# Small products of two heads interleaved on the two halves of the TensorE array, in a two-layer hybrid decoder kernel

## The chip, the cores and the metric

The kernel runs on one core of one Trainium2 chip. Its time is the device time of one execution in microseconds (us), the median of several runs. A profile of one more execution gives the rows that are read below; there, PE is TensorE's matrix products, PEld its weight loads, DVE is VectorE, ACT is ScalarE, POOL is GpSimd and SP is the queue that issues the transfers.

## The reference, cut to what matters

Two layers of a decoder for 256 tokens of width 1024. In each layer four token mixers work on one projected input, and each has four heads of 64 channels:

```
xn = rmsnorm(h);  u_nsa, u_hgrn, u_ret, u_rwkv = split(xn @ w_in)
nsa:   per head, scores q.k against 16 compressed blocks, 256 selected and 256 window keys;
       three softmaxes, each with a causal mask, times their values
hgrn:  S_t = diag(f_t) S_(t-1) + k_t^T v_t ;  o_t = q_t S_t        (per head, 64 x 64 state)
ret:   (q k^T * decay) v                                            (per head)
rwkv:  S_t = S_(t-1)(diag(w_t) - kk^T (kk a)) + v_t^T k_t ; y_t = S_t r_t
h = h + (sum_m sigmoid(xn @ w_gate[m]) * (mixer_m @ w_branch[m])) @ w_out
h = h + (silu(hn @ w_ffn_gate) * (hn @ w_ffn_up)) @ w_ffn_down
h = h + sigmoid(hp @ w_ple_gate) * (p @ w_ple_proj)
```

## The kernel before

Channels lie on the 128 partitions and tokens along the free side; a chunk of 128 channels holds two heads, the even head (`hp` = 0) on partitions 0 to 63 and the odd one (`hp` = 1) on 64 to 127. There are two kinds of products.

The **big products** (lines L222 to L224, L264 to L266, L440 to L442) are the projections: each float32 weight block is loaded, split into a high and a low part by ACT (L207) and DVE (L208), and multiplied in three products of 128x128 weights with 256 columns. They need nothing of the mixers except at a few places, and fill TensorE for most of the time.

The **small products** are the mixers' own, in float32. All of them are issued by the helper `matmul` or `transpose` of `Front` and so carry its line, L141 (L144 issues nothing itself). A float32 product that is no transpose runs as two records in the trace. A small product uses a part of the array, given by `tile_position`: rows (the partitions of its operands) and columns (the partitions of its result). A product of 64 channels uses one half of the rows; one whose result is on 64 partitions, one half of the columns; one with both, a quarter.

The order of the instructions on each engine is made when the kernel is built, by a scheduler with priorities: there are three lanes, "G" for the big products, "A" for rwkv and "B" for ret, hgrn and nsa. `Front` puts a small product 100000 ahead in priority, so that it goes before any big product once the scheduler takes it for ready. On the chip each engine runs its list in order. Results go to 8 PSUM banks: two named `pA` (lane A), three `pB` (lane B), three `mm` (big products). A new tile of a name waits for one of its banks to be read out.

The small products that the change touches, in the order of a layer: in `rwkv` the sums of squares `pk` (two products of 32 result rows), the four chunk products per head into `pa` (`[128, 4, 128]`, one bank a head), and the transposed values `pv` (8 products on the halves of the columns, the four of one half first); in `hgrn` the blocks of `hgrn_blocks` (8 quarter products a head, called once with 64 columns and three times, over `hq`, with 96), four quarter products a head into `pp`, and two of 128 columns a head into `pp` for the off-diagonal part; in `nsa` the scores of a head (`nsa_scores`: bank `pb` with 272 and 16 columns, each a product and then a mask added by a bfloat16 product of `nmx` with the identity on the whole array; bank `pa` with two products of 256 columns and a mask), and the eight transposes of `nsa_turn`.

Of the kernel before, what the change touches and what calls it, by code (L numbers as in the profile page):

```python
# [32 lines left out]
P = 128  # L33
# [96 lines left out]
class Front:  # L130
# [7 lines left out]
    def _issue(self, f, *args, **kw):  # L138
        p = self.tc.cur_priority
        self.tc.cur_priority = p - self.AHEAD  # L140
        f(*args, **kw)  # L141
        self.tc.cur_priority = p + 1

    def matmul(self, *args, **kw):  # L144
        self._issue(self.nc.tensor.matmul, *args, **kw)

    def transpose(self, *args, **kw):
        self._issue(self.nc.tensor.transpose, *args, **kw)


class Trunk:
# [372 lines left out]
    def rwkv(self, l, ums):  # L524
# [44 lines left out]
        for j in range(2):  # L569
            self.pe.matmul(pk[32 * j:32 * j + 32], self.hsel, sq[:, j], start=True, stop=True, tile_position=(0, 32 * j))  # L570
# [37 lines left out]
        for j in range(2):  # L608
            for hp in range(2):
                h = 2 * j + hp  # L610
                hr = slice(hp * 64, hp * 64 + 64)
                pa = self.ps([P, 4, 128])
                for c in range(4):
                    self.pe.matmul(pa[:, c], bk[c % 2][hr, j, c // 2].rearrange("p x t -> p (x t)"),
                                     ar[c % 2][hr, j, c // 2].rearrange("p x t -> p (x t)"), start=True, stop=True)
# [58 lines left out]
        for par in range(2):  # L674
            for cp in range(2):
                c = 2 * cp + par
                for j in range(2):
# [122 lines left out]
    def hgrn(self, l, tm, zs):  # L800
# [32 lines left out]

        for hp in range(2):
            pp = self.ps([P, 4, 64])
            self.hgrn_blocks(hp, k, lambda jc, x: q[64 * hp:64 * hp + 64, jc // 2, (jc % 2) * P + 64 * x:(jc % 2) * P + 64 * x + 64], pp)
            V.tensor_mul(cd[hp], pp, self.id64[:, None, :].to_broadcast([P, 4, 64]))
# [4 lines left out]
        for i, m in enumerate(QUADS):  # L842
# [25 lines left out]
            V.tensor_mul(quad(kn)[:, :, :3], kb[:, :, :3], bc(post))  # L868
            for hp in range(2):
                pp = self.ps([P, 4, 96])  # L870
                self.hgrn_blocks(hp, k, lambda jc, x: qq[64 * hp:64 * hp + 64, 2 * jc + x], pp)
# [6 lines left out]

        for hp in range(2):
            hr = slice(hp * 64, hp * 64 + 64)  # L880
            pp = self.ps([P, 2, 2, 64])
            for jc in range(4):
                j, c = jc // 2, jc % 2
                self.pe.matmul(pp[:64, j, c], k[hr, j, c * P:c * P + 64], q[hr, j, c * P + 64:c * P + P],
                                 start=True, stop=True, tile_position=(64 * hp, 0))
            nc.scalar.activation(at[hp][:64, :, :, 64:], pp[:64], AF.Copy)
# [10 lines left out]
        V.tensor_mul(half(kn)[:, :, 0], half(k)[:, :, 0], bc(1))  # L897
        for hp in range(2):
            hr = slice(hp * 64, hp * 64 + 64)
            pp = self.ps([P, 2, P])  # L900
            for j in range(2):
                self.pe.matmul(pp[:, j], kn[hr, j, :P], qn[hr, j, P:], start=True, stop=True)
            nc.scalar.activation(ato[:, hp], pp, AF.Copy)
# [3 lines left out]
    def hgrn_blocks(self, hp, k, q, out):  # L907

        for jc in range(4):
            for x in range(2):  # L910
                ts = slice((jc % 2) * P + 64 * x, (jc % 2) * P + 64 * x + 64)
                self.pe.matmul(out[64 * x:64 * x + 64, jc], k[64 * hp:64 * hp + 64, jc // 2, ts], q(jc, x),
                                      start=True, stop=True, tile_position=(64 * hp, 64 * x))
# [66 lines left out]
    def nsa(self, l, tm, vc, ksw, q):  # L980
# [6 lines left out]
        es, ts = [], []  # L987
        for step in "ssTsTpsTTp":
# [10 lines left out]

# [49 lines left out]
    def nsa_turn(self, ea, e2, ec):  # L1049
# [6 lines left out]
        for br in range(2):  # L1056
            self.pe.transpose(p2[:, br], ea[:, 1, br], self.ident)
# [412 lines left out]
```

## Time and profile before

| | us |
|---|---|
| median of 3 runs | 1031.58 (1031.05 to 1031.73) |
| the profiled execution | 1034.5 |
| its span, first to last instruction | 1032.7 |
| PE busy in the span | 1016.8 (98%), 9548 products |
| DVE busy | 770.4 (75%) |
| ACT busy | 541.1 (52%) |
| mean granted TensorE clock | 0.993 |

A busy figure is the time that an engine's records cover. Records of PE overlap, as a product is in flight while the next begins; the time that a product holds up its followers is therefore read from start to start, not from its length. The mixers of the first layer lie between 35 and 216 us of the span, those of the second between 542 and 724.

### The profile page before, as it was taken

To read this page: it belongs to the slowest core of one execution; us is meant where nothing else is said; L and a number is where in the kernel's file an instruction comes from. 1 tells how busy PE (TensorE), PEld (TensorE's weight loads), DVE (VectorE), ACT (ScalarE), POOL (GpSimd) and SP (SyncE) were. 2 spreads that over 40 slices of the span, in tenths; PEclk is the share of its full clock that TensorE was granted. 3 is DMA by queue.
4 is the path that set the end of the run, shared out by engine and by line. 5 is a ranking of instruction groups with operands and counts; after the bars stand their busy time and mean duration, and the time that the engine had idled before them with its cause. 6 is when DMAs were issued, how large, how long until landed. Compare 5 with 4: busy or idle time off the path is not lost.

```text
span 1032.7 us, 22828 instructions
## 1 busy us (share of the span) xinstructions
PE 1016.8 (98%) x9548; PEld 976.8 (95%) x9548; DVE 770.4 (75%) x1337; ACT 541.1 (52%) x863; POOL 7.6 (1%) x28
## 2 busy tenths in 40 slices
PE   8999999999999999999999999999999999999996
PEld 8988988899999999999998989988999999999996
DVE  6888968687787777656767889576777777776566
ACT  6643554565664544455545545546456544544444
POOL 0000000000000000000000000000000000000000
PEclk9999999999999999999989999999999999999998
DMA  8654333246665666666644553333566666666661
GB/s 289 188 198 146 103 104 94 91 155 201 186 203 182 189 197 192 185 192 197 181 157 126 184 165 104 101 105 93 172 200 181 182 192 196 193 196 184 191 184 55
DMA packets 50502, 171.33 MB, mean 166 GB/s; under 512 B 5856, under 2 KB 6624, under 8 KB 50272
## 3 DMA queue, kind: packets, MB, share of 16 engines
q1 hardware_dynamic: 50112, 169.76, 53.8%
q8 instruction: 75, 1.23, 0.5%
q14 instruction: 27, 0.22, 0.1%
q10 hardware_dynamic: 288, 0.11, 0.0%
HBM read 168.80 MB, written 1.05 MB: 164 GB/s over the span
## 4 chain that ended last, share of the span: by engine, by line
PE 88%; DVE 7%; DMA 2%; issue 2%; ACT 1%; SPq 0%; DVEq 0%; ACTq 0%
PE mm L222 22%; PE mm L223 21%; PE mm L224 21%; PE pB L141 6%; PE pA L141 5%; DVE wl L208 2%; PE pA L222 2%; PE pA L223 2%; PE pA L224 2%; DMA T<-in_w_cmp_dram 1%; PE pA L264 1%; PE pA L265 1%; PE pA L266 1%; DMA cst<-in_consts_dram 1%; PE pB L364 1%
## 5 line engine op out<-in xcount | busy, mean ns | idle before, releaser
L207 ACT ACTIVATE wh<-wr 128x1024 fp32r<-128x1024 f32 (+3 forms) x314 | 325.8, 1040 | 355.1 <-PE mm L224 223.9
L208 DVE TENSOR_TENSOR wl<-wr,wh 128x1024 fp32r<-128x1024 f32 (+3 forms) x314 | 375.0, 1196 | 143.2 <-ACT wh L207 141.4
L222 PE MATMUL mm<-xh,wl 128*128 128x256 f32 x1472 | 411.8, 280 | 0.9 <-DVE lbw L1186 0.7
L224 PE MATMUL mm<-xh,wh 128*128 128x256 f32 x1472 | 410.6, 279 | 0.0
L223 PE MATMUL mm<-xl,wh 128*128 128x256 f32 x1472 | 410.6, 279 | 0.0
L222 PEld LDWEIGHTS mm<-xh,wl 128*128 128x128 f32 x1472 | 276.7, 188 | 4.4 <-issue 1.4
L223 PEld LDWEIGHTS mm<-xl,wh 128*128 128x128 f32 x1472 | 276.6, 188 | 2.9 <-issue 2.1
L224 PEld LDWEIGHTS mm<-xh,wh 128*128 128x128 f32 x1472 | 276.8, 188 | 2.5 <-issue 1.4
L222 PE MATMUL mm<-A,wl 128*128 128x256 f32 x332 | 91.8, 277 | 0.0
L223 PE MATMUL mm<-A,wh 128*128 128x256 f32 x332 | 91.8, 277 | 0.0
L224 PE MATMUL mm<-A,wh 128*128 128x256 f32 x332 | 91.8, 277 | 0.0
L222 PEld LDWEIGHTS mm<-A,wl 128*128 128x128 f32 x332 | 62.5, 188 | 0.0
L224 PEld LDWEIGHTS mm<-A,wh 128*128 128x128 f32 x332 | 62.3, 188 | 0.0
L223 PEld LDWEIGHTS mm<-A,wh 128*128 128x128 f32 x332 | 62.3, 188 | 0.0
L141 PE MATMUL pA<-A,A 64*64 64x64 f32 (+3 forms) x1008 | 49.7, 223 | 1.1 <-DVE A L648 1.1
L141 PEld LDWEIGHTS pA<-A,A 64*64 64x64 f32 (+3 forms) x1008 | 41.6, 135 | 8.8 <-DVE A L648 1.5
L222 PE MATMUL mm<-Y,wl 128*128 128x256 f32 x160 | 44.7, 279 | 0.0
L223 PE MATMUL mm<-Y,wh 128*128 128x256 f32 x160 | 44.4, 277 | 0.0
L224 PE MATMUL mm<-Y,wh 128*128 128x256 f32 x160 | 44.2, 276 | 0.0
L1230 DVE TENSOR_TENSOR T<-mm,rstd 128x512 f32<-128x512 f32 x32 | 22.1, 689 | 13.9 <-PE mm L224 13.9
L1233 ACT ACTIVATE T<-T,vech 128x256 f32<-128x256 f32 x64 | 28.8, 500 | 2.6 <-DVE T L1230 2.6
L222 PEld LDWEIGHTS mm<-Y,wl 128*128 128x128 f32 x160 | 30.1, 188 | 0.0
(388 smaller groups left out, 1612.5 us busy)
## 6 DMA issues: line engine op xcount, KB each, us to landing
wr<-in_w_gate_dram SPq DMA_DIRECT2D x64, 512.0 KB, 3.7
wr<-in_w_fm_dram SPq DMA_DIRECT2D x46, 512.0 KB, 4.3
wr<-in_w_fg_dram SPq DMA_DIRECT2D x44, 512.0 KB, 4.2
wr<-in_w_fu_dram SPq DMA_DIRECT2D x44, 512.0 KB, 4.1
wr<-in_w_fd_dram SPq DMA_DIRECT2D x32, 512.0 KB, 3.8
wr<-in_w_branch_dram SPq DMA_DIRECT2D x16, 512.0 KB, 4.3
wr<-in_w_out_dram SPq DMA_DIRECT2D x16, 512.0 KB, 4.1
wr<-in_w_pg_dram SPq DMA_DIRECT2D x16, 512.0 KB, 4.2
```

The costliest lines, as they stand in the source:

```text
L141: f(*args, **kw)
L207: nc.scalar.activation(hi[:, s], raw[:, s], AF.Copy)
L208: nc.vector.tensor_sub(lo[:, s], raw[:, s], hi[:, s])
L222: mm(out, wlo, xhi, start=start, stop=False)
L223: mm(out, whi, xlo, start=False, stop=False)
L224: self.last_mm = mm(out, whi, xhi, start=False, stop=stop)
L264: mm(ps[:, c], lo, xs[k][0], start=c == 0 and k == 0, stop=False, skip_group_check=True)
L265: mm(ps[:, c], hi, xs[k][1], start=False, stop=False, skip_group_check=True)
L266: mm(ps[:, c], hi, xs[k][0], start=False, stop=k == n - 1, skip_group_check=True)
L364: nc.tensor.matmul(ps[:, tc_:tc_ + 1], a[:, tc_ * P:(tc_ + 1) * P], self.inv_dm, start=i == 0 and tc_ == 0, stop=i == n - 1, skip_group_ch ...
L1230: self.nc.vector.tensor_mul(th, ps, self.rstd_b)
L1233: self.nc.scalar.activation(th[:, c], th[:, c], AF.Tanh, scale=0.5, bias=self.vech[l][:, col:col + 1])
```

## The change

`Front.together` issues a list of products as one group: the first is issued, and the scheduler is told to take the others right after it. The lists go through both heads in turn (odd head, even head, odd head, ...), each head into a bank of its own, and begin with the product whose operand is made last. `hgrn_blocks` now makes both heads' blocks and returns both banks. The `pv` products change halves of the columns with each product. In nsa the bank `pb` is started once, by the 272-column product, where it was started twice; the 16-column product and the two masks follow; this opening part, now `nsa_first`, is made for head h+1 in one list with the rest of head h. The transposes of `nsa_turn` are one list. No product, no shape and no operation of another engine is added or removed.

```
     def matmul(self, *args, **kw):
-        self._issue(self.nc.tensor.matmul, *args, **kw)
+        return self._issue(self.nc.tensor.matmul, *args, **kw)
...
+    def together(self, steps):
+
+        head = steps[0]()
+        with self.tc.issue_after(head.ins):
+            for f in steps[1:]:
+                f()
...
         pk = self.ps([64, T])
-        for j in range(2):
-            self.pe.matmul(pk[32 * j:32 * j + 32], self.hsel, sq[:, j], start=True, stop=True, tile_position=(0, 32 * j))
+        self.pe.together([functools.partial(self.pe.matmul, pk[32 * j:32 * j + 32], self.hsel, sq[:, j], start=True, stop=True,
+                                            tile_position=(0, 32 * j)) for j in (1, 0)])
...
         for j in range(2):
+
+            pas = [self.ps([P, 4, 128]) for _ in range(2)]
+
+            def chunk(c, hp):
+                hr = slice(hp * 64, hp * 64 + 64)
+                return self.pe.matmul(pas[hp][:, c], bk[c % 2][hr, j, c // 2].rearrange("p x t -> p (x t)"),
+                                      ar[c % 2][hr, j, c // 2].rearrange("p x t -> p (x t)"), start=True, stop=True)
+
+            self.pe.together([functools.partial(chunk, c, hp) for c in (3, 0, 1, 2) for hp in (1, 0)])
             for hp in range(2):
...
-        for par in range(2):
-            for cp in range(2):
-                c = 2 * cp + par
-                for j in range(2):
+        for cp in range(2):
+            for j in range(2):
+                for par in range(2):
+                    c = 2 * cp + par
...
-        for hp in range(2):
-            pp = self.ps([P, 4, 64])
-            self.hgrn_blocks(hp, k, lambda jc, x: ..., pp)
+        pps = self.hgrn_blocks(k, lambda hr, jc, x: ..., 64)
...
+            pps = self.hgrn_blocks(k, lambda hr, jc, x: qq[hr, 2 * jc + x], 96)
...
+        pps = [self.ps([P, 2, 2, 64]) for _ in range(2)]
+        steps = []
+        for jc in range(4):
+            j, c = jc // 2, jc % 2
+            for hp in (1, 0):
+                hr = slice(hp * 64, hp * 64 + 64)
+                steps.append(functools.partial(self.pe.matmul, pps[hp][:64, j, c], k[hr, j, c * P:c * P + 64],
+                                               q[hr, j, c * P + 64:c * P + P], start=True, stop=True, tile_position=(64 * hp, 0)))
+        self.pe.together(steps)
...
+        pps = [self.ps([P, 2, P]) for _ in range(2)]
+        steps = []
+        for j in range(2):
+            for hp in (1, 0):
+                hr = slice(hp * 64, hp * 64 + 64)
+                steps.append(functools.partial(self.pe.matmul, pps[hp][:, j], kn[hr, j, :P], qn[hr, j, P:], start=True, stop=True))
+        self.pe.together(steps)
...
+    def hgrn_blocks(self, k, q, n):
+
+        pps = [self.ps([P, 4, n]) for _ in range(2)]
+        steps = []
         for jc in range(4):
             for x in range(2):
                 ts = slice((jc % 2) * P + 64 * x, (jc % 2) * P + 64 * x + 64)
+                for hp in (1, 0):
+                    hr = slice(64 * hp, 64 * hp + 64)
+                    steps.append(functools.partial(self.pe.matmul, pps[hp][64 * x:64 * x + 64, jc], k[hr, jc // 2, ts], q(hr, jc, x),
+                                                   start=True, stop=True, tile_position=(64 * hp, 64 * x)))
+        self.pe.together(steps)
+        return pps
...
+    def nsa_first(self, h, ksw, q, beside=()):
+
+        j, hr = h // 2, slice((h % 2) * 64, (h % 2) * 64 + 64)
+        pb = self.ps([P, 512])
+        mm = lambda o, w, x, start=False, stop=False: functools.partial(self.pe.matmul, o, w, x, start=start, stop=stop,
+                                                                        skip_group_check=True)
+        steps = [mm(pb[:, :272], q[hr, j, :P], ksw[hr, :272], start=True), *beside[:1],
+                 mm(pb[:, 272:288], q[hr, j, P:], ksw[hr, :16]), *beside[1:],
+                 mm(pb[:, :272], self.identb, self.nmx[:, 16:]),
+                 mm(pb[:, 272:288], self.identb, self.nmx[:, :16], stop=True)]
+        self.pe.together(steps)
+        return pb
...
-        mm(pb[:, :272], q[hr, j, :P], ksw[hr, :272], start=True, stop=False, skip_group_check=True)
-        mm(pb[:, :272], self.identb, self.nmx[:, 16:], start=False, stop=True, skip_group_check=True)
-        mm(pb[:, 272:288], q[hr, j, P:], ksw[hr, :16], start=True, stop=False, skip_group_check=True)
-        mm(pb[:, 272:288], self.identb, self.nmx[:, :16], start=False, stop=True, skip_group_check=True)
...
+        if h < 3:
+            self.first = self.nsa_first(h + 1, ksw, q, steps)
+        else:
+            self.pe.together(steps)
...
+        self.pe.together([tr(p2[:, 1], ea[:, 1, 1]), tr(p2[:, 0], ea[:, 1, 0]), *(tr(p2[:, 2 + c], ec[:, c]) for c in range(2)),
+                          *(tr(p1[:, br, 0], e2[:, br]) for br in range(2)), *(tr(p1[:, br, 1], ea[:, 0, br]) for br in range(2))])
```

What this makes of the order on TensorE is shown at three places of the first layer. A row is one product, or several of the same that follow each other; the numbers behind a name tell tiles apart, and the size is that of the result.

In hgrn, the second use of `hgrn_blocks` on `hq`, on TensorE before (`pB_267` is the even head's bank, `pB_268` the odd one's; `pA` is rwkv, `mm` big products):

```order
L440 MATMUL mm_239_1874<-wl242_1908,xh_173 128x256
L441 MATMUL mm_239_1874<-wh242_1907,xl_174 128x256
L141 MATMUL pA_96_800<-A_95_798,A_92_777 64x64 x16
L141 MATMUL pB_267_2010<-hq_261_1990,B_247_1949 64x96 x8
L141 MATMUL pB_268_2022<-hq_261_1990,B_247_1949 64x96 x8
L442 MATMUL mm_239_1874<-wh242_1907,xh_173 128x256
```

and the same place now:

```order
L142 MATMUL pA_96_800<-A_95_798,A_92_777 64x64 x16
L142 MATMUL pB_268_2011<-hq_261_1990,B_247_1949 64x96
L142 MATMUL pB_267_2010<-hq_261_1990,B_247_1949 64x96
L142 MATMUL pB_268_2011<-hq_261_1990,B_247_1949 64x96
L142 MATMUL pB_267_2010<-hq_261_1990,B_247_1949 64x96
L142 MATMUL pB_268_2011<-hq_261_1990,B_247_1949 64x96
L142 MATMUL pB_267_2010<-hq_261_1990,B_247_1949 64x96
L142 MATMUL pB_268_2011<-hq_261_1990,B_247_1949 64x96
L142 MATMUL pB_267_2010<-hq_261_1990,B_247_1949 64x96
L142 MATMUL pB_268_2011<-hq_261_1990,B_247_1949 64x96
L142 MATMUL pB_267_2010<-hq_261_1990,B_247_1949 64x96
```

The sixteen products of two heads stood one head behind the other and now take turns; the place among the big products is the same.

In rwkv, the chunk products of the second pair of heads (`pA_77` is the even head's bank, `pA_78` the odd one's; `mm` are big products), on TensorE before:

```order
L141 MATMUL pA_77_664<-A_65_620,A_67_622 128x128
L141 MATMUL pA_77_664<-A_66_621,A_68_623 128x128
L141 MATMUL pA_77_664<-A_65_620,A_67_622 128x128
L141 MATMUL pA_77_664<-A_66_621,A_68_623 128x128
L222 MATMUL mm_209_1558<-xh_173,wl210_1561 128x256
L223 MATMUL mm_209_1558<-xl_174,wh210_1560 128x256
L224 MATMUL mm_209_1558<-xh_173,wh210_1560 128x256
L222 MATMUL mm_209_1558<-xh_173,wl210_1561 128x256
L223 MATMUL mm_209_1558<-xl_174,wh210_1560 128x256
L224 MATMUL mm_209_1558<-xh_173,wh210_1560 128x256
L141 MATMUL pA_78_677<-A_65_620,A_67_622 128x128
```

and now:

```order
L142 MATMUL pA_78_665<-A_66_621,A_68_623 128x128
L142 MATMUL pA_78_665<-A_65_620,A_67_622 128x128
L142 MATMUL pA_78_665<-A_66_621,A_68_623 128x128
L142 MATMUL pA_78_665<-A_65_620,A_67_622 128x128
L233 MATMUL mm_209_1558<-xl_174,wh210_1560 128x256
L234 MATMUL mm_209_1558<-xh_173,wh210_1560 128x256
L232 MATMUL mm_209_1558<-xh_173,wl210_1561 128x256
L142 MATMUL pA_77_664<-A_66_621,A_68_623 128x128
L142 MATMUL pA_77_664<-A_65_620,A_67_622 128x128
L142 MATMUL pA_77_664<-A_66_621,A_68_623 128x128
L142 MATMUL pA_77_664<-A_65_620,A_67_622 128x128
L233 MATMUL mm_209_1558<-xl_174,wh210_1560 128x256
```

The two heads still stand apart, with big products between them: the odd head now goes first and the even head three big products later. (For the first pair of heads, whose two banks are both free, the built order does take turns; and the two `pk` products, which had one big product between them, now follow each other.)

In nsa, the scores of the first head, on TensorE before (`pB_309` is `pb`, `pB_308` is `pa`):

```order
L141 MATMUL pB_301_2200<-cst_155,B_300_2198 128x128 x4
L141 MATMUL pB_309_2218<-ns_ksw_207_1552,U_208_1557 128x272
L141 LDWEIGHTS identb_516
L141 MATMUL pB_309_2218<-nmx_518,identb_516 128x272
L141 MATMUL pB_309_2218<-ns_ksw_207_1552,U_208_1557 128x16
L141 LDWEIGHTS identb_516
L141 MATMUL pB_309_2218<-nmx_518,identb_516 128x16
L141 MATMUL pB_308_2217<-ns_ksw_207_1552,U_208_1557 128x256 x2
L141 LDWEIGHTS identb_516
L141 MATMUL pB_308_2217<-nmx_518,identb_516 128x256
```

and now (`pB_308` is `pb` of the first head, `pB_310` that of the second):

```order
L142 MATMUL pB_301_2200<-cst_155,B_300_2198 128x128 x4
L142 MATMUL pB_308_2217<-ns_ksw_207_1552,U_208_1557 128x272
L142 MATMUL pB_308_2217<-ns_ksw_207_1552,U_208_1557 128x16
L142 LDWEIGHTS identb_516
L142 MATMUL pB_308_2217<-nmx_518,identb_516 128x272
L142 LDWEIGHTS identb_516
L142 MATMUL pB_308_2217<-nmx_518,identb_516 128x16
L142 MATMUL pB_310_2223<-ns_ksw_207_1552,U_208_1557 128x272
L142 MATMUL pB_310_2223<-ns_ksw_207_1552,U_208_1557 128x16
L142 LDWEIGHTS identb_516
L142 MATMUL pB_310_2223<-nmx_518,identb_516 128x272
L142 MATMUL pA_127_987<-A_111_905,A_113_920 64x64 x4
```

The two score products of a bank now stand together, with its two masks behind them. The first head's bank `pa` has moved from behind the masks to two big products later, past the second head's opening. The odd heads' openings take turns with the rest of the head before only for the last pair, heads 2 and 3; for the others the built order keeps the two parts apart.

## Rows read from the trace of the kernel before

**Rows 1.** The page, its parts on busy time (engine, us, share of the span, instructions) and on the chain of work that ended last (share of the span by engine).

```profile
PE 1016.8 (98%) x9548; PEld 976.8 (95%) x9548; DVE 770.4 (75%) x1337; ACT 541.1 (52%) x863; POOL 7.6 (1%) x28
...
PE 88%; DVE 7%; DMA 2%; issue 2%; ACT 1%; SPq 0%; DVEq 0%; ACTq 0%
```

**Rows 2.** The waits of TensorE over the whole span: who waited for whom, us in total, times, longest.

```profile
PE mm L141 <- DMA T<-in_w_cmp_dram: 1.9, 2, 1.0
...
PE pA L141 <- DVE A L648: 1.1, 2, 0.6
```

**Rows 3.** Busy time of each engine in stretches of the span (start and end, length; then per engine us busy and instructions, the granted TensorE clock, DMA share, GB/s). The first four lie in the first layer's mixers, the last two are the same places of the second layer as the first two.

```profile
75.00:95.00 20.00, 18.92 (x197) 17.01 (x196) 19.78 (x47) 9.42 (x14) 0.00 (x0) 1.00 0.50 173
115.00:135.00 20.00, 19.43 (x340) 18.15 (x339) 19.81 (x49) 10.83 (x25) 0.30 (x1) 1.00 0.30 96
135.00:155.00 20.00, 20.00 (x285) 17.77 (x279) 10.64 (x26) 12.80 (x26) 0.00 (x0) 1.00 0.33 99
155.00:215.00 60.00, 60.00 (x521) 52.14 (x520) 45.20 (x117) 32.91 (x89) 0.00 (x0) 1.00 0.34 101
583.00:603.00 20.00, 18.99 (x199) 17.16 (x199) 19.75 (x47) 9.42 (x14) 0.00 (x0) 1.00 0.52 174
623.00:643.00 20.00, 19.49 (x350) 18.17 (x348) 19.85 (x50) 11.08 (x25) 0.30 (x1) 1.00 0.33 99
```

**Rows 4.** The order of time on TensorE, small products of 64 rows by 128 columns with 256 moving columns (start, us until the last end, line, names, weights rows*columns, result, type, records): in rwkv, where rows 0 to 63 and 64 to 127 take turns, and in nsa, where all four records use one half. A row's start to the next row's start is what it takes.

```profile
40.22 1.14 PE L141 MATMUL pA<-A,sm 64*128 64x256 f32 x8
41.28 0.38 PE L223 MATMUL mm<-xl,wh 128*128 128x256 f32 x1
...
167.12 1.13 PE L141 MATMUL pB<-ns_ksw,U 64*128 64x256 f32 x4
168.18 0.28 PE L141 MATMUL pB<-nmx,identb 128*128 128x256 bf16 x1
```

**Rows 5.** The order of time on TensorE at the two `pk` products.

```profile
49.48 0.28 PE L222 MATMUL mm<-xh,wl 128*128 128x256 f32 x1
...
50.23 0.38 PE L223 MATMUL mm<-xl,wh 128*128 128x256 f32 x1
50.55 0.62 PE L141 MATMUL pA<-A,cst 128*32 128x256 f32 x2
51.10 0.38 PE L224 MATMUL mm<-xh,wh 128*128 128x256 f32 x1
51.32 0.29 PE L222 MATMUL mm<-xh,wl 128*128 128x256 f32 x1
```

**Rows 6.** The order of time on TensorE at the chunk products of the first pair of heads (`pA<-A,A`), among products of ret on halves of the columns (`pB<-tm,B`), and at those of one later head.

```profile
71.83 0.28 PE L223 MATMUL mm<-xl,wh 128*128 128x256 f32 x1
72.03 0.80 PE L141 MATMUL pB<-tm,B 128*64 128x64 f32 x18
72.76 0.49 PE L141 MATMUL pA<-A,A 64*128 64x128 f32 x4
...
75.36 0.38 PE L224 MATMUL mm<-xh,wh 128*128 128x256 f32 x1
...
78.75 1.16 PE L141 MATMUL pA<-A,A 64*128 64x128 f32 x8
79.84 0.38 PE L222 MATMUL mm<-xh,wl 128*128 128x256 f32 x1
```

**Rows 7.** The order of time on TensorE at three groups of quarter products: hgrn with 64 columns, hgrn over `hq` with 96, and rwkv's 32x32 products with the idle time before them and what ended it.

```profile
115.99 0.97 PE L141 MATMUL pB<-B,B 64*64 64x64 f32 x32
116.89 0.38 PE L442 MATMUL mm<-wh,xh 128*128 128x256 f32 x1
...
122.42 1.22 PE L141 MATMUL pB<-hq,B 64*64 64x96 f32 x31
123.57 0.39 PE L442 MATMUL mm<-wh,xh 128*128 128x256 f32 x1
...
134.66 0.69 PE L141 MATMUL pA<-A,A 32*32 32x32 f32 x32 [0.57 <-DVE A L648]
135.28 0.39 PE L222 MATMUL mm<-xh,wl 128*128 128x256 f32 x1
```

**Rows 8.** The order of time on TensorE where hgrn ends: `pv` (`pA<-cst,A 128*64`), the rest of the third `hq` group, the odd head's quarter products `pp` (`pB<-B,B 64*64`) and the off-diagonal part of the odd head (`64*128`).

```profile
140.48 1.58 PE L141 MATMUL pA<-cst,A 128*64 128x128 f32 x16
141.99 0.62 PE L141 MATMUL pB<-hq,B 64*64 64x96 f32 x9
...
142.53 0.24 PE L141 MATMUL pB<-hq,B 64*64 64x96 f32 x1
...
142.62 0.24 PE L141 MATMUL pB<-hq,B 64*64 64x96 f32 x1
...
143.56 0.68 PE L141 MATMUL pB<-B,B 64*64 64x64 f32 x8
144.17 0.39 PE L223 MATMUL mm<-xl,wh 128*128 128x256 f32 x1
...
147.47 0.71 PE L141 MATMUL pB<-B,B 64*128 64x128 f32 x4
148.11 0.69 PE L141 MATMUL pA<-A,A 128*64 128x64 f32 x16
```

**Rows 9.** The order of time on TensorE at the opening of nsa's first head: its first product; the opening with both products and both masks lasts until the 256-column products of group 4 begin.

```profile
165.81 0.72 PE L141 MATMUL pB<-ns_ksw,U 64*128 64x272 f32 x2
```

More of the change, by code (lines that the diff above doesn't have):

```diff
@@ L608, in rwkv @@
         for j in range(2):
+            pas = [self.ps([P, 4, 128]) for _ in range(2)]
[4 more added lines that the diff above has]
+            self.pe.together([functools.partial(chunk, c, hp) for c in (3, 0, 1, 2) for hp in (1, 0)])
             for hp in range(2):
-                h = 2 * j + hp
+                h, pa = 2 * j + hp, pas[hp]
                 hr = slice(hp * 64, hp * 64 + 64)
[L612 to L615, printed above, removed]
                 for par in range(2):
@@ L877, in hgrn @@
             q, k = qn, kn
-        for hp in range(2):
[L880 to L886, printed above, removed]
+        pps = [self.ps([P, 2, 2, 64]) for _ in range(2)]
[7 more added lines that the diff above has]
+        self.pe.together(steps)
+        for hp in range(2):
+            nc.scalar.activation(at[hp][:64, :, :, 64:], pps[hp][:64], AF.Copy)
             for x in range(2):
@@ L897, in hgrn @@
         V.tensor_mul(half(kn)[:, :, 0], half(k)[:, :, 0], bc(1))
-        for hp in range(2):
[L899 to L903, printed above, removed]
+        pps = [self.ps([P, 2, P]) for _ in range(2)]
[5 more added lines that the diff above has]
+        self.pe.together(steps)
+        for hp in range(2):
+            nc.scalar.activation(ato[:, hp], pps[hp], AF.Copy)
         sms = [(at[h % 2][:, h // 2, 0], ato[:, h % 2, h // 2], at[h % 2][:, h // 2, 1]) for h in range(4)]
         return self.tm_out(l, sms, tm, EPS, False, "Y1", V_HN, None, s2)
-    def hgrn_blocks(self, hp, k, q, out):
+    def hgrn_blocks(self, k, q, n):
+        pps = [self.ps([P, 4, n]) for _ in range(2)]
+        steps = []
         for jc in range(4):
@@ L987, in nsa @@
         es, ts = [], []
+        self.first = self.nsa_first(0, ksw, q)
         for step in "ssTsTpsTTp":
@@ L1052, in nsa_turn @@
         p1, p2 = self.ps([P, 2, 2, P]), self.ps([P, 4, P])
-        for br in range(2):
-            self.pe.transpose(p1[:, br, 0], e2[:, br], self.ident)
-            self.pe.transpose(p1[:, br, 1], ea[:, 0, br], self.ident)
-        for br in range(2):
-            self.pe.transpose(p2[:, br], ea[:, 1, br], self.ident)
-        for c in range(2):
-            self.pe.transpose(p2[:, 2 + c], ec[:, c], self.ident)
+        tr = lambda o, x: functools.partial(self.pe.transpose, o, x, self.ident)
+        self.pe.together([tr(p2[:, 1], ea[:, 1, 1]), tr(p2[:, 0], ea[:, 1, 0]), *(tr(p2[:, 2 + c], ec[:, c]) for c in range(2)),
+                          *(tr(p1[:, br, 0], e2[:, br]) for br in range(2)), *(tr(p1[:, br, 1], ea[:, 0, br]) for br in range(2))])
         ta = self.g([P, 2, 2, P])
```

23 lines of the change are left out of this document (11 added, 12 removed).

## Prediction

> **What bounds the kernel now.** Read first the page's busy times and its chain: TensorE is busy 98% of the span and makes up 88% of the chain, so what it does not have to do comes off the end, unless it then waits [rows 1]. Then TensorE's waits: those that belong to the mixers are few, 1.9 us for the compression weights' transfer and 1.1 us for DVE in an rwkv group, both layers together [rows 2]. Then the engines by stretch. In the first layer DVE is busy 19.78 of 20 us between 75 and 95, and 19.81 of 20 between 115 and 135; the second layer shows 19.75 and 19.85 at the same places. Between 135 and 155 it is busy 10.64 of 20, and between 155 and 215 45.20 of 60 [rows 3]. So TensorE's time is the bound in the later mixers, and in the two tight stretches DVE is one as well. The granted clock is 1.00, the level of 2.4 GHz, in all of these.
>
> **What taking turns is worth.** Eight rwkv records of 256 columns that take turns on the two halves of the rows need 41.28 - 40.22 = 1.06 us until the next product; four nsa records of the same size, all on one half, need 168.18 - 167.12 = 1.06 us [rows 4]. The second half is free. This is the measured form of what the change does, with the same weights (64x128), so I take it for all groups that really take turns, and half the time is the bound that no group can beat.
>
> **The terms, for one layer**, each from start to start. An ordinary big product follows the one before it by 0.11 us (an estimate from the 0.11 to 0.12 between the big products' starts where no small one lies between).
>
> *pk.* From the big product at 49.48 to the one at 51.32 it is 1.84 us, with two visits to small products [rows 5]. One visit: 0.75 (49.48 to 50.23), then 0.22 for the next big one (51.10 to 51.32) and 0.11 for the last: 1.08. The two products go to different columns, so the second is taken as free beside the first. Saved 0.76; if it is not free, 0.24 less, by the 0.55 to 0.75 of a visit.
>
> *Chunk products, first pair of heads.* 71.83 to 75.36, 3.53 us, holds these 16 records and 40 of ret in turns [rows 6]. Sixteen that take turns should need what eight of one head need: 79.84 - 78.75 = 1.09 and 0.20 to enter. The 40: 18 took 0.73, of which 0.20 is the change to another tile size, so 0.029 each, 1.17, and 0.20 to enter and to leave. Together 2.86, less 0.11 as the two groups now have one more big product between them: saved 0.78 here. In the second layer the order still has one mixed visit; I take 0.7 for the mean. The second pair of heads stands apart in the new order, odd head first, even head later: 0.
>
> *hgrn, 64 columns.* 32 records in 0.90 us [rows 7], eight on each quarter of the array. Eight records on one quarter alone take 144.17 - 143.56 = 0.61 [rows 8]. If the quarters are independent, 0.29 is saved.
>
> *hgrn over hq, first and second.* 31 records from 122.42 to 123.57, 1.15 us [rows 7]. On one quarter they follow at 0.09 (142.53, 142.62) [rows 8]; eight are 0.10 + 7 x 0.085, and 0.17 to leave: an estimate of 0.8. Saved 0.4 each, 0.8.
>
> *The end of hgrn.* `pv`: 16 records in 141.99 - 140.48 = 1.51 us, one half of the columns after the other [rows 8]. In turns they are eight at 0.109 (1.51 less 0.20 to leave, over the some 12 that did not overlap) and 0.20: 1.07, saved 0.44. `pp`: the odd head's run of 0.61 lies beside the even head's, saved 0.6. Off-diagonal: 148.11 - 147.47 = 0.64 for the odd head, saved 0.64 [rows 8]. Against it, the new order cuts `pp` into pieces among products of other tile sizes; two extra changes at some 0.15 to 0.2. Net 1.35, bounds 0.9 and 1.7.
>
> *nsa.* Opening a bank takes 167.12 - 165.81 = 1.31 us now [rows 4, 9], with four changes between half and whole array. With one change: 0.33 for a 272-column record, 0.23 for the other, 0.24 for the two small ones and 0.22 for the masks, 1.0; these parts are estimates, 256 columns on one half being 0.22 apart by [rows 4]. Saved 0.3 a head, 1.2. Heads 2 and 3 alone take turns, which puts most of the 1.06 of four 256-column records beside the opening: 0.8. Some gathered transposes: 0.2. Sum 2.2, bounds 1.2 and 2.6.
>
> Sum: 0.76 + 0.7 + 0.29 + 0.8 + 1.35 + 2.2 = 6.1 us a layer, 12.2 in both.
>
> **The rule on weight loads** bears on `pv`. The trace: 18 ret records in turns on two halves of the columns, with all rows, came at 0.029 us after the change of size is taken off [rows 6], below the 0.109 of one half [rows 8]; so loads on the other half of the columns do overlap. The Trainium skill, TensorE: Matmul & The Clock Gate, Part 3 (The mechanism), says that a weight load overlaps a running product only when its row group differs. By that rule `pv` gains nothing and the time would be 0.9 us later over two layers. The trace disagrees, and the sum goes by the trace.
>
> **What is given back.** The stretch from 115 to 135 cannot get shorter than DVE's work in it, 19.81 of 20 us [rows 3]. The two gains there (hgrn 64 columns, hq: 1.1 us) I count as lost to waits on DVE's masks and copies, such as the 0.57 us before the 32x32 products [rows 7]; bounds nothing and all of it. The 1.46 of `pk` and the chunks fall before the stretch from 75 to 95; TensorE comes earlier to a transfer that it already waits for and to a DVE that is full. But DVE has some slack before 75, and the transfer is set off by TensorE's own progress: of 1.46 I take 0.2 as lost (bounds 0 and 1.46). After 135 DVE is half idle and nothing is given back. So 1.3 a layer, 2.6 in both.
>
> 12.2 - 2.6 = 9.6 us. The profiled execution took 1034.5 us, which gives 1024.9; the median of the runs shown is 2.9 lower, and the same saving gives 1031.58 - 9.6 = **1022.0**. With the bounds that are likely together (gain 11 to 13.5, given back 1 to 4.5) the forecast spans 1019 to 1025.
>
> **The rivals.** *Nothing is given back* (0.15): DVE works ahead once results come sooner; the 0.57 us wait was one place only. 1031.6 - 12.2 = 1019.4, and 1018.2 with the upper bound of nsa.
>
> *Banks* (0.17): a group takes two or three banks at once. Lane A has two, lane B three, and a new tile waits until one is read. In nsa all three are taken by `pb` and `pa` of one head and `pb` of the next, so transposes and the next scores wait for the softmax. For it: the order that keeps the second pair of chunk products apart. Against: PE never idles in 155 to 215 [rows 3], where big products fill the holes. Beside it stands a page: the Trainium skill, TensorEngine Tiling (Array Packing), Gotcha 1: PSUM Pressure, states that row tiles write to different banks and that row tiling raises the pressure on PSUM; no run here shows it yet. If nsa's 2.2 and all before 135 but 1.0 go, 1.0 + 1.35 a layer are left: 4.7 in both, 1026.9.
>
> *No change* (0.04): the halves do not run beside each other and only visits saved count; `pk` 0.76 a layer, less waits: 1030 to 1032. [rows 4] speaks against it.
>
> *Slower* (0.05): TensorE's list is in order, and a group begins with the product that is ready last. If the real operand comes later than the scheduler took it to, everything queued behind waits: big products, and with them DVE's and ACT's next results. There are about 17 groups a layer, 34 in all; at 0.28 us more wait each the 9.6 is gone, at 0.36 the time is 1034.2. In the tight stretches this is plausible; elsewhere [rows 2] shows no such waits.
>
> **The numbers.** Forecast 0.59. Faster by over 0.2% (2 us, about what a measurement of this kernel can tell from no change): 0.59 + 0.15 + 0.17 = 0.91. Same 0.04, slower 0.05. The range takes in the first two rivals, 1018.2 and 1026.9, and leaves out about 0.1.
>
> **What would show it.** In the profile after: `pB<-hq,B` groups of 32 records at about 0.8 us; `pB<-B,B 64*128` with eight records in 0.64; nsa's opening at 1.0; the first pair of chunk products 16 records in 1.1; TensorE idle before small products near 115 to 135 longer than the 0.57 us, with DVE named. It is wrong if groups of turns show twice the length of one head, if TensorE waits for DVE or ACT between 155 and 215, or if the big products start later there than the list before would have them.

## The result and the profile after

The changed kernel takes 1024.34 us (median of four executions, 1022.4 to 1027.5) against 1031.65 in the runs beside it: ratio 0.9932, 95% interval 0.9915 to 0.9949, 7.3 us less. Forecast were 1022.0, with a range of 1018.2 to 1026.9. The profiled execution took 1024.59 us, span 1022.8.

The page after, busy time and chain, answers [rows 1]; the waits of TensorE below it (who waited for whom, us in total, times, longest) answer [rows 2]:

```profile
PE 1008.8 (99%) x9548; PEld 975.6 (95%) x9548; DVE 769.3 (75%) x1337; ACT 539.9 (53%) x863; POOL 7.3 (1%) x28
...
PE 89%; DVE 7%; issue 1%; DMA 1%; ACT 1%; DVEq 0%; ACTq 0%
```

```profile
PE pA L142 <- DVE A L663: 1.5, 1, 1.5
...
PE pB L142 <- DVE hq L866: 0.5, 1, 0.5
PE mm L142 <- DMA T<-in_w_cmp_dram: 0.4, 1, 0.4
...
PE pA L142 <- ACT A L674: 0.3, 1, 0.3
```

TensorE is as full as before. Its waits on the mixers came to 1.9 and 1.1 us; now they are 1.5, 0.5, 0.4 and 0.3, a little less in sum, but elsewhere: the compression weights are waited for 1.5 us less, and VectorE 0.9 us more, of whose 2.0 us now 1.48 stand at one place. The stretches that answer [rows 3]:

```profile
115.00:135.00 20.00, 18.52 (x299) 17.52 (x294) 19.81 (x55) 10.85 (x24) 0.30 (x1) 0.96 0.36 107
155.00:215.00 60.00, 60.00 (x538) 54.61 (x537) 46.89 (x119) 34.81 (x90) 0.00 (x0) 1.00 0.36 109
623.00:643.00 20.00, 19.12 (x325) 17.68 (x324) 19.88 (x52) 10.88 (x25) 0.30 (x1) 1.00 0.35 108
```

Between 155 and 215 TensorE never idles (60.00 of 60), so no bank leaves it without work there; before, it did not idle there either. Between 115 and 135 VectorE is busy 19.81 of 20 us, as before, and TensorE now only 18.52. The order of time on TensorE at the groups of [rows 5 to 9]:

```profile
49.08 0.28 PE L232 MATMUL mm<-xh,wl 128*128 128x256 f32 x1
49.28 0.63 PE L142 MATMUL pA<-A,cst 128*32 128x256 f32 x4
49.84 0.38 PE L233 MATMUL mm<-xl,wh 128*128 128x256 f32 x1
50.06 0.28 PE L234 MATMUL mm<-xh,wh 128*128 128x256 f32 x1
50.18 0.29 PE L232 MATMUL mm<-xh,wl 128*128 128x256 f32 x1
...
72.30 1.16 PE L142 MATMUL pA<-A,A 64*128 64x128 f32 x16
73.39 0.38 PE L233 MATMUL mm<-xl,wh 128*128 128x256 f32 x1
...
112.99 0.70 PE L142 MATMUL pB<-B,B 64*64 64x64 f32 x32
113.61 0.38 PE L452 MATMUL mm<-wh,xh 128*128 128x256 f32 x1
...
119.24 0.83 PE L142 MATMUL pB<-hq,B 64*64 64x96 f32 x29
120.00 0.39 PE L452 MATMUL mm<-wh,xh 128*128 128x256 f32 x1
...
131.70 0.69 PE L142 MATMUL pA<-A,A 32*32 32x32 f32 x32 [1.48 <-DVE A L663]
132.33 0.39 PE L232 MATMUL mm<-xh,wl 128*128 128x256 f32 x1
...
138.86 1.09 PE L142 MATMUL pA<-cst,A 128*64 128x128 f32 x16
139.88 0.47 PE L142 MATMUL pB<-hq,B 64*64 64x96 f32 x11
...
163.08 0.85 PE L142 MATMUL pB<-ns_ksw,U 64*128 64x272 f32 x4
...
164.09 0.49 PE L142 MATMUL pB<-ns_ksw,U 64*128 64x272 f32 x1
```

```profile
145.60 0.97 PE L142 MATMUL pB<-B,B 64*64 64x64 f32 x10
146.50 0.39 PE L233 MATMUL mm<-xl,wh 128*128 128x256 f32 x1
```

The row at 145.60 merges two records of `pp` with the eight of the off-diagonal part, the first of which starts at 145.86. The sizes of the groups measured here are those of the forecast to 0.05 us:

| | before | forecast | after |
|---|---|---|---|
| `pk`, big product to third big product | 1.84 | 1.08 | 1.10 (49.08 to 50.18) |
| 16 chunk products | in a 3.53 mix | 1.09 | 1.09 (72.30) |
| hgrn, 64 columns | 0.90 | 0.61 | 0.62 (112.99) |
| hgrn over `hq` | 1.15 for 31 records | 0.8 | 0.76 for 29 (119.24) |
| `pv` | 1.51 | 1.07 | 1.02 (138.86) |
| off-diagonal part, both heads | 0.64 each | 0.64 | 0.64 (145.86 to 146.50) |
| opening of nsa, first head | 1.31 | 1.0 | 1.01 (163.08) |

**What the mixers gained.** Two marks bound each layer's mixers: the first rwkv product and the first product of the output projection, both layers, before and then after. The same number of TensorE products lies between them in both kernels, 2466 in the first layer and 2478 in the second:

```profile
284.46 0.28 PE L264 MATMUL mm<-A,wl 128*128 128x256 f32 x1
...
546.66 1.14 PE L141 MATMUL pA<-A,sm 64*128 64x256 f32 x8
...
792.20 0.28 PE L264 MATMUL mm<-A,wl 128*128 128x256 f32 x1
```

```profile
39.44 1.14 PE L142 MATMUL pA<-A,sm 64*128 64x256 f32 x8
...
279.79 0.28 PE L274 MATMUL mm<-A,wl 128*128 128x256 f32 x1
...
540.33 1.14 PE L142 MATMUL pA<-A,sm 64*128 64x256 f32 x8
...
782.52 0.28 PE L274 MATMUL mm<-A,wl 128*128 128x256 f32 x1
```

Before, with 40.22 from [rows 4], the layers take 244.2 and 245.5 us; after, 240.4 and 242.2. Two things lie in the second pair that are not the mixers' work. Windows of after (columns as in [rows 3]; the number after PE's busy time is the count of products, those that run over an edge included), and below them the last of these of before:

```profile
132.00:134.00 2.00, 2.00 (x37) 1.96 (x30) 2.00 (x7) 1.07 (x2) 0.00 (x0) 0.81 0.44 180
134.00:136.00 2.00, 2.00 (x11) 2.00 (x11) 2.00 (x5) 1.07 (x3) 0.00 (x0) 0.50 0.01 4
136.00:138.00 2.00, 2.00 (x28) 1.68 (x27) 1.75 (x4) 0.90 (x1) 0.00 (x0) 0.84 0.47 104
745.00:765.00 20.00, 20.00 (x172) 20.00 (x172) 15.30 (x19) 9.60 (x13) 0.00 (x0) 1.00 0.67 203
```

```profile
745.00:765.00 20.00, 20.00 (x179) 20.00 (x178) 15.40 (x19) 9.84 (x13) 0.00 (x0) 1.00 0.68 209
```

First, behind the wait of 1.48 us at 131.70 the granted clock is 0.50, the level of 1.2 GHz, for 3.4 us (11 products in 2 us): 1.7 us lost. Second, from 722, where the second layer's last small product lies, to 808 the big products follow each other at 0.118 us and not 0.113, at a granted clock of 1.00 and without a wait: 172 in 20 us against 179. Below, this spacing is called the step of the big products. Up to the mark at 782.5 this costs (782.5 - 721.9) / 0.1178 x 0.0045 = 2.3 us. Without both, and without 0.1 us for a short stretch of the same slow step behind the first layer's last small product, the mixers take 238.5 and 239.9: 5.7 us less in each layer, where 6.1 less 1.3 was forecast. The kernel gained more than forecast in its mixers and lost some of it elsewhere.

### The profile page after: what moved, and what is told of

It reads as the page before. It is cut to its first block, busy times and chain, and to the rows that moved or that the text cites. A ratio compares the mean times of both kernels' runs of the same rounds, so it can differ in the third digit from the quotient of the medians.

```text
span 1022.8 us, 22822 instructions
## 1 busy us (share of the span) xinstructions
PE 1008.8 (99%) x9548; PEld 975.6 (95%) x9548; DVE 769.3 (75%) x1337; ACT 539.9 (53%) x863; POOL 7.3 (1%) x28
## 4 chain that ended last, share of the span: by engine, by line
PE 89%; DVE 7%; issue 1%; DMA 1%; ACT 1%; DVEq 0%; ACTq 0%
PE mm L233 23%; PE mm L232 22%; PE mm L234 22%; PE pB L142 5%; PE pA L142 4%; DVE wl L218 2%; PE pA L232 2%; PE pA L233 2%; PE pA L234 2%; PE pA L274 1%; PE pA L275 1%; PE pA L276 1%; DMA T<-in_w_cmp_dram 1%; PE pB L374 1%; PE mm L452 1%
## 5 line engine op out<-in xcount | busy, mean ns | idle before, releaser
L233 PEld LDWEIGHTS mm<-Y,wh 128*128 128x128 f32 x160 | 30.1, 188 | 0.5 <-issue 0.4
```

The costliest lines, as they stand in the source:

```text
L233: mm(out, whi, xlo, start=False, stop=False)
```

## The experiments

The table gives for each run the median, the mean granted clock of all timed executions, the time between the two marks (less such half-clock time, and less what the step of 0.118 adds behind the last small product), and where that step follows the mixers. For the kernel before, the clock is the mean over the executions timed beside these runs. How far a layer's time can be trusted is told by programs that are alike up to its end: the first layers of changed, x1 and x5 take 238.5, 239.0 and 239.1, those of before and x6 244.2 and 244.0, the second layers of changed and x1 239.9 and 239.4. A difference of 0.6 us in one layer therefore says nothing.

| | median us | clock | layer 1 | layer 2 | step 0.118 behind the mixers |
|---|---|---|---|---|---|
| before | 1031.58 | 0.9947 | 244.2 | 245.5 | no |
| changed | 1024.34 | 0.9918 | 238.5 | 239.9 | layer 2 |
| x1 the same again | 1024.33 | 0.9933 | 239.0 | 239.4 | layer 2 |
| x2 heads in sequence | 1022.58 | 0.9944 | 241.4 | 240.5 | no |
| x3 nsa as before | 1027.07 | 0.9918 | 240.8 | 242.3 | no |
| x4 blocks in sequence | 1024.14 | 0.9942 | 239.8 | 239.5 | layer 1 |
| x5 tiny product | 1020.50 | 0.9945 | 239.1 | 239.9 | ended at 724 |
| x6 tiny product in before | 1032.01 | 0.9945 | 244.0 | 245.9 | no |
| x7 tail on GpSimd | 1017.50 | 0.9952 | 237.3 | 239.3 | no |
| x8 x7, heads in sequence | 1024.33 | 0.9937 | 239.9 | 239.5 | layer 1 |
| x9 x7, nsa as before | 1024.95 | 0.9945 | 240.5 | 242.2 | no |
| x10 before, tail on GpSimd | 1030.38 | 0.9945 | 243.3 | 245.3 | no |

**x1, the changed kernel again.** No edit.

> The changed kernel once more, for its spread. Its four executions so far took 1022.4, 1024.1, 1024.6 and 1027.5 us at mean granted clocks of 0.994, 0.992, 0.992 and 0.989. Theory one (clock steps): the program itself takes 1022.4, and each stretch of 3.41 us at a granted clock of 0.50, as the one behind the 1.48 us wait at 131.70, adds 1.7 us and takes 0.0017 off the mean clock; the new times then stand at 1022.4 plus a multiple of 1.7, each with the clock that belongs to it, and the kernel before, at 1031.05 to 1031.9, shows few such steps. Theory two (plain noise, or waits for transfers of differing length): times are spread evenly and don't go with the mean clock.

1024.33 us, ratio 0.9928 (0.9912 to 0.9943). The six times, 1022.1 to 1025.8, fall in the order of their mean clocks, 0.996 to 0.991, but not in clean steps of 1.7. So the clock makes most of the spread: 0.001 of it goes with some 1.0 us in the four executions of the changed kernel above (1022.4 at 0.994 to 1027.5 at 0.989) and with some 0.7 in these six. The wait of 1.48 us is there again, at 132.73, and this time nothing follows it; the step of 0.118 is there again:

```profile
132.80:136.00 3.20, 3.20 (x54) 3.16 (x55) 3.20 (x11) 1.87 (x4) 0.00 (x0) 1.00 0.36 133
745.00:765.00 20.00, 20.00 (x172) 20.00 (x171) 14.84 (x19) 9.76 (x13) 0.00 (x0) 1.00 0.65 198
```

**x2, the odd head's products first, then the even head's.**

```
-            self.pe.together([functools.partial(chunk, c, hp) for c in (3, 0, 1, 2) for hp in (1, 0)])
+            self.pe.together([functools.partial(chunk, c, hp) for hp in (1, 0) for c in (3, 0, 1, 2)])
...
```

and so in `hgrn_blocks`, `pp`, the off-diagonal part and `pv`.

> As the changed kernel, with the same lists and banks, but in every list of rwkv and hgrn the odd head's products stand first and then the even head's; pv goes half by half as before. nsa keeps its new order. Theory (taking turns is what pays): the groups return to their old lengths, chunk products 0.7, hgrn over 64 columns 0.29, over hq 0.8, pv 0.44, pp and off-diagonal 1.24 less the 0.33 of cuts, 3.1 us a layer; up to 1.1 of that stays hidden behind VectorE in 115 to 135. So 4 to 6.3 us slower than the changed kernel: 1026.5 to 1028.7 without clock steps. Rival (the order of the lists, the banks and the single visits pay, the halves of the array do not run beside each other): within 1 us of the changed kernel, 1022 to 1025.

1022.58 us, ratio 0.9912 (0.9898 to 0.9926): by the time, the rival's number. The order of time and a window speak otherwise:

```profile
120.82 1.23 PE L142 MATMUL pB<-hq,B 64*64 64x96 f32 x30
121.98 0.39 PE L452 MATMUL mm<-wh,xh 128*128 128x256 f32 x1
...
138.66 1.58 PE L142 MATMUL pA<-cst,A 128*64 128x128 f32 x16
140.18 0.30 PE L142 MATMUL pB<-hq,B 64*64 64x96 f32 x2
```

```profile
745.00:765.00 20.00, 20.00 (x179) 20.00 (x178) 15.55 (x19) 10.27 (x13) 0.00 (x0) 1.00 0.64 202
```

The groups have their old lengths (1.16 and 1.52 us), and between the marks x2 is 2.7 us slower than the mean of changed and x1 in the first layer and 0.9 in the second, 3.6 in all, a little under the 4 that the theory asked for at least; that the second layer gives so much less is not explained. (Of the waits in the first layer, the one for the compression weights is 0.9 us longer in x2 than in changed and x1, the one at the 32x32 group 0.9 us shorter.) But its big products leave the second layer at 0.113 (179 in 20 us), which gives 2.3 us to the mark and some 1 behind it, and its mean clock is 0.0017 higher than that of changed and x1 together (0.9927), some 1.7 us. The time alone would have condemned the part of the change that works.

**x3, nsa as before**: `nsa`, `nsa_scores` and `nsa_turn` of the kernel before.

> As the changed kernel, with nsa as it was before: a bank opened twice, no list over two heads, transposes in the old order. Theory: nsa's part is worth 2.2 us a layer (bounds 1.2 and 2.6), so the time is 4.4 us longer, 1026.8 without clock steps, bounds 1024.8 and 1027.6. Rival (banks: three taken at once hold up the softmax and give the gain back): no longer than the changed kernel, 1022.4 to 1024.4.

1027.07 us, ratio 0.9961 (0.9947 to 0.9976). Between the marks it is 4.7 us slower than the mean of changed and x1 (2.1 and 2.6), as the theory has it; the median shows 2.7 of them, as no step of 0.118 follows its second layer. The rival of the banks falls.

**x4, `hgrn_blocks` head after head**: only its loops change places, `for hp in (1, 0)` outermost.

> As the changed kernel, but in hgrn_blocks alone the odd head's eight products stand first and then the even head's, so these groups take 0.9 and 1.15 us again instead of 0.62 and 0.8, and in 115 to 135 TensorE has 1.1 us more work a layer. Theory (this gain is given back, as VectorE is full in that stretch): the wait of 1.48 us at the 32x32 group shrinks by some 0.9 and the time stays where it is, 1022.4 within 0.5 without clock steps, with no stretch at a granted clock of 0.50 behind that wait. Rival (the gain reaches the end): 1.1 to 1.5 us a layer slower, 1024.6 to 1025.4. The third hq group lies behind 135 and costs 0.3 a layer by both.

1024.14 us, ratio 0.9926 (0.9912 to 0.9939), the same as changed. Between the marks it is 1.0 slower in the first layer, 0.2 faster in the second. Some 1.4 us a layer of work for TensorE, 2.8 in all, cost 0.9 in both layers together, and 0.6 of that was expected from the third `hq` group, which lies behind the tight stretch: in the tight stretch the gain is given back, as forecast. No wait at the 32x32 group is left in its list of waits. The step of 0.118 stands behind the first layer here (218 to 312), not behind the second.

**x5, one tiny product**, an existing helper called once more:

```
             ps = self.ps([P, 2, T], "mm")
+            (l, m, p) == (1, 3, 1) and self.quarter(ps)     # in gates()
```

> As the changed kernel, with one product more: in the second layer, some 31 big products behind the last small product of nsa (at about 726), a 64x64 product of 2 columns whose result is overwritten, as the kernel already issues one in the feed-forward part. In the changed kernel the big products follow each other at 0.118 us from 722 to 808, at 0.113 in the kernel before over the same work; the granted clock is 1.00 in both. In the kernel before, the tiny product at 330.22 ends such a stretch (0.118 ahead of it, 0.113 behind) and holds up the stream by 0.42 us itself. Theory (the stream of big products has two steady steps, and which one it leaves the mixers with is chance): from 726 on the step is 0.113; 82 us / 0.1178 x 0.0045 = 3.1 us saved, less 0.4: 2.7 us faster than the changed kernel, 1021.6 in the median. Rival (the step is set by where the operands or banks lie): 0.118 comes back at once, and the time is 0.4 longer, 1024.7.

1020.50 us, ratio 0.9903 (0.9890 to 0.9917), 3.8 us faster than changed. The order of time at the tiny product, and the window:

```profile
723.76 0.28 PE L234 MATMUL mm<-xh,wh 128*128 128x256 f32 x1
723.97 0.27 PE L240 MATMUL mm<-cst 64*64 64x2 f32 x2
724.17 0.39 PE L232 MATMUL mm<-xh,wl 128*128 128x256 f32 x1
724.39 0.28 PE L233 MATMUL mm<-xl,wh 128*128 128x256 f32 x1
...
726.79 0.28 PE L233 MATMUL mm<-xl,wh 128*128 128x256 f32 x1
726.90 0.28 PE L234 MATMUL mm<-xh,wh 128*128 128x256 f32 x1
727.01 0.28 PE L232 MATMUL mm<-xh,wl 128*128 128x256 f32 x1
```

```profile
745.00:765.00 20.00, 20.00 (x179) 20.00 (x178) 15.10 (x17) 10.36 (x14) 0.00 (x0) 1.00 0.68 214
```

Ahead of 723.97 the step is 0.118; from 724.9 on it is 0.113, and it stays so. The rival falls: same operands, same banks, other step. Of the 3.8 us some 2.7 are the step's; the rest goes with the clock (0.9945), which the tiny product has no reason to raise; four executions do not tell more.

**x6, the same tiny product in the kernel before.**

> The kernel before with the same tiny product at the same place of its program; there the big products already follow each other at 0.113. Theory of two steady steps: nothing to mend; 0.4 us slower than before if the step stays at 0.113, and 2 us more if the tiny product itself turns it to 0.118 until 792. Rival (the tiny product saves time by something else, as a bank or a queue): faster than before by 2 to 3 us here too.

1032.01 us, ratio 1.0010 (1.0001 to 1.0019): nothing to mend there, and it costs what it takes, 0.4 us between the marks of the second layer. So x5's gain is no general gift of that product.

**x7, four elementwise operations of hgrn on GpSimd.**

```
-            V.tensor_mul(quad(qn)[:, :, 1:], qb[:, :, 1:], bc(pre))
+            (G if i == 2 else V).tensor_mul(quad(qn)[:, :, 1:], qb[:, :, 1:], bc(pre))
```

and so for `quad(kn)`, `half(qn)` and `half(kn)` (the last two in every case).

> As the changed kernel, but the four elementwise products of hgrn's last level and of its off-diagonal part (L880 and L882 for the third level, L912, L914; 0.55, 0.55, 0.43 and 0.42 us on VectorE) are made by GpSimd, three of which stand on VectorE ahead of the rwkv operation that the 32x32 group waits 1.48 us for. The scheduler puts that group two big products earlier. Theory (what is given back in 115 to 135 is VectorE's work, and the long wait brings a stretch at a granted clock of 0.50): the wait falls to 0 to 0.4 us, no stretch at 0.50 behind it, the mean clock of the executions rises by 0.001 towards that of the kernel before, and the first layer's mixers end 1 to 1.5 us earlier, 2 to 3 in the executions that had the slow stretch; median 1021.5 to 1023 if the step of the big products behind 722 stays as it is. Rival (GpSimd is too slow, and hgrn's products wait for it instead): waits named after GpSimd at pp or the off-diagonal products, and no gain.

1017.50 us, ratio 0.9879 (0.9864 to 0.9894), the fastest version: 6.8 us below changed, 14 below before. The 32x32 group, one of the operations on GpSimd (busy us, mean ns), and the window:

```profile
130.74 0.69 PE L142 MATMUL pA<-A,A 32*32 32x32 f32 x32 [0.48 <-DVE A L663]
```

```profile
L882 POOL TENSOR_TENSOR B<-B,B 128x384 f32<-128x384 f32 x2 | 2.6, 1310 | 0.2
```

```profile
745.00:765.00 20.00, 20.00 (x179) 20.00 (x178) 13.32 (x15) 10.62 (x15) 0.00 (x0) 1.00 0.65 208
```

The wait is 0.48 instead of 1.48, no wait of TensorE is named after GpSimd, so that rival falls, and the mixers' marks lie 1.4 and 0.4 us closer than in the mean of changed and x1. The step behind the second layer is 0.113 without a tiny product (some 3 us), and the clock is 0.9952 (2.5 us). The first part was designed and a rise of the clock by 0.001 expected; the step was luck. With the slow step the median would be some 1020.8, a little below the 1021.5 to 1023 expected.

**x8 and x9, x7 with heads in sequence, and x7 with nsa as before.**

> The kernel of x7 (four operations on GpSimd), and the lists of rwkv and hgrn head after head as in x2. x7 took 1017.5 us, with the big products at 0.113 behind both layers' mixers and no stretch at a granted clock of 0.50 ahead of the tail. Theory (taking turns pays in the groups; in x2 a better step and one slow stretch less hid it): by the first big products behind the mixers of each layer, x2 stood 2.4 us behind the changed kernel in the first layer and 0.7 to 1.6 in the second; so 4 us slower than x7, 1021.5, if step and clock are those of x7, and up to 4 more if a slow step returns; counted ahead of the big products that follow the mixers the difference is 2 to 3 us a layer. Rival (turns are worth nothing at the end of the kernel): within 1 us of x7.

> The kernel of x7 with nsa as before. Theory: nsa's part is worth 2.2 us a layer, 1021.9 in all, if the step of the big products behind the mixers stays at 0.113. Rival (x3 stood only 2.7 us behind the changed kernel, so nsa is worth 1.35 a layer, bounds 1.2 and 2.6): 1020.2.

x8: 1024.33 us, ratio 0.9941 (0.9926 to 0.9955), 6.8 us slower than x7, of which 2.8 lie between the marks (2.6 and 0.2). In the first layer the rival falls; in the second turns pay next to nothing, where 2 to 3 us were expected. Part of the reason stands in x7's list of waits, and in x8's there is no such line:

```profile
PE pB L142 <- DVE B L889: 1.0, 1, 1.0
```

With turns, TensorE comes to the second layer's `hq` group at 635.90 early and waits 0.97 us for VectorE; x8, 0.8 us behind x7 ahead of that wait, is level with it behind. The rest is open. The step of 0.118 follows its first layer from 218 to 312, (312 - 218) / 0.1178 x 0.0045 = 3.6; the clock is 0.0015 lower.

x9: 1024.95 us, ratio 0.9945 (0.9929 to 0.9961); 3.2 and 2.9 us between the marks, with the same step as x7, 6.1 in all. Both theories expected less from nsa (4.4 and 2.7).

**x10, the four operations on GpSimd in the kernel before.**

> The kernel before with the same four operations on GpSimd, to tell what these give without the change. There the 32x32 group waits 0.57 us in the first layer and 0.51 in the second. Theory (VectorE's work in 115 to 135 matters only as far as TensorE waits for it): at most these 1.1 us, 1030 to 1031; so nearly all of the 14 us between before and x7 is the change's own. Rival (GpSimd's help is what makes x7 fast): 1026 or less.

1030.38 us, ratio 0.9993 (0.9982 to 1.0004): 0.9 and 0.2 us less between the marks, which is what the two waits of [rows 2] on VectorE took; neither is in x10's list. So GpSimd's help is not what makes x7 fast, and the rival falls. Between the marks it is worth 1.1 us here and 1.8 in the changed kernel, a difference too near the scatter to show that the change makes it worth more.

## Why the prediction was right, and what it missed

**Right: the sign, the range, and each group's size.** The table of groups shows most of the terms one by one; `pp` and nsa's heads 2 and 3, whose products stand among others now, are not in it. That products on two halves of the columns run beside each other with all rows is shown by `pv`: 1.02 us for 16 records in turns, 1.51 before and 1.52 in x2 with one half after the other. The Trainium skill, TensorE: Matmul & The Clock Gate, Part 3 (The mechanism), says that a weight load overlaps only when its row group differs; by that `pv` would have stayed at 1.51, and the trace disagrees.

**By parts.** Of the 11.4 us between the marks, turns in rwkv and hgrn make 3.6 by x2 (2.8 by x8 against x7), nsa 4.7 by x3 (6.1 by x9 against x7). If the parts add up, 3.1 are left, which no run took apart; the rows show 0.74 a layer of them at `pk`. Turns pay 2.7 and 2.6 in the first layer but 0.9 and 0.2 in the second: but for the chunk products no term of the forecast let the layers differ.

**Right: VectorE takes back what is gained in 115 to 135.** The 1.1 us a layer were counted as lost there, and x4 shows that they nearly are. x7 shows the cause: with three operations less ahead of it on VectorE, the 32x32 group waits 1.0 us less.

**Wrong sign: the gains ahead of 75.** 0.2 us a layer were put down as lost to the compression weights and VectorE. The wait for those weights fell from 1.9 to 0.4 us over both layers. In the second layer that is firm: 0.8 to 0.9 us in before, x6 and x10, none of 0.2 or more in any kernel with the change. In the first part of it is scatter: x6, there the same program as before, waits 0.47 where before waits 1.04, and x2 waits 1.34. Why the transfer comes earlier against TensorE was not tried.

**Too small: nsa.** 2.2 us a layer were forecast; x3 gives 2.4, which the scatter does not tell from it, x9 3.1. The first head's opening has its forecast length, so a surplus would lie in what follows it; which part is open.

**The rivals.** *Banks* falls by x3 and x9: nsa's part is worth 4.7 and 6.1 us, where the rival had all of it lost. The missing idle time in 155 to 215 alone would not have decided it, as big products fill holes there. *Nothing given back* falls by x4 and by the wait of 1.48 us, and not by the sum: 11.4 is nearer its 12.2 than the 9.6 forecast. *Slower* falls by the time; 1.48 us is the only long wait that a group brought.

**Two slips in the sums.** For `hq`, 0.10 + 7 x 0.085 + 0.17 makes 0.87, not 0.8; that the measured 0.76 lies near the 0.8 is luck. The rival's lower end, 1031.6 - 12.2 less 0.4 a layer, is 1018.6, not 1018.2.

**Missed: two losses that no term held.** The sum forecast 9.6 us; the mixers gave 11.4 (mean of changed and x1). Then came the step of 0.118 behind the second layer, (808 - 722) / 0.1178 x 0.0045 = 3.3 us, where the kernel before has about 1.0 of the same (792 to 818): 2.3 more. And the mean clock fell from 0.9947 to 0.9927, 0.0020 x 1020 = 2.0 us (an estimate; by the slopes seen in x1, 1.4 to 2.0). 11.4 - 2.3 - 2.0 = 7.1, measured 7.3. So the median comes within 2.3 us of 1022.0 by two errors of opposite sign, 1.8 more from the mixers and 4.3 lost elsewhere: that is luck.

**Open.** That the long wait lowers the clock is supported, not shown: a stretch at 0.50 followed it in two of the four profiles with that wait (changed and x3, not x1 and x5), and the mean clocks of the kernels that have it are 0.9918, 0.9933 and 0.9918, but 0.9945 in x5, against 0.9937 to 0.9952 in those without. Behind a wait of 0.6 us between 507 and 515, which all twelve profiles have, stretches at 0.50 between 511 and 523 appear in those of before, changed, x1, x3, x4, x6, x8 and x10, not in x2, x5, x7 and x9. What decides the step with which big products leave the mixers is open as well; it is the same in both profiles of the same program.

## What to carry to other kernels

Groups of small products on parts of the array can be priced from the trace of a neighbour group that already takes turns; these prices held to 0.05 us. Where the other engine is full, first ask who is late then: the next gain here lay in moving 2 us of elementwise work a layer off VectorE, worth 1.8 us between the marks. A difference of a few us in a median says nothing of a part until the step of the big products and the mean clock are the same in both kernels: set marks in the trace around the part, see that the same number of products lies between them, compare between them, and learn the scatter from two profiles of one program.

## What the runs showed of the hardware

A stream of equal products (128x128 weights, 256 columns) has two steady steps at the same granted clock of 1.00, 0.113 and 0.118 us. The slow one lasted 94 us in x4, over many weight and operand tiles, the fast one longer; a 64x64 product of 2 columns that interrupts it by 0.4 us turned the slow step into the fast one within six products (x5), and left the fast one as it was (x6). The two such products that every kernel has in its feed-forward parts (in the kernel before at 330 and 839) have 0.118 ahead of them and 0.113 behind them in all twelve profiles. The Trainium skill, TensorE: Matmul & The Clock Gate, Back-to-back issue gap, says that in a stream of loads and products both set the spacing, and gives columns / 2.4 + 2.5 ns for a product by itself, by which an estimate for 256 columns is 109 ns; the trace shows neither step there, and no run tells why there are two.

One elementwise product of 128x384 (L882) took 0.54 to 0.55 us on VectorE in the changed kernel. On GpSimd, in x7, it took 1.78 us in the first layer and 0.84 in the second, which makes the mean of 1.31 above; no run tells why the same operation has two times there.
